# A hybrid transformer trunk on one core: VectorE and ScalarE in written order, with lower parts, conv taps and output copies placed later

## The chip, the cores and the metric

The kernel runs on one core of one Trainium2 chip. The metric is the device time of one execution in microseconds (us), taken as the median of several runs. TensorE multiplies matrices; VectorE, ScalarE and GpSimd work element by element; SyncE issues the loads. A matmul writes into one of eight PSUM banks, all other tiles are in SBUF.

## The reference, cut to what matters

A trunk of two layers on 16 meta tokens and 256 tokens (272 columns), model width 1024, all float32. Each layer is feed-forward, mixer, feed-forward, each with a norm before and after it. The mixer of layer 0 is a gated short convolution, that of layer 1 differential attention.

```python
def swiglu(h, w_gu, w_down):
    g, u = jnp.split(h @ w_gu, 2, axis=-1)        # w_gu 1024 x 5632
    return (jax.nn.silu(g) * u) @ w_down          # w_down 2816 x 1024

def short_conv_mixer(h, w_in, conv_w, w_out):
    b, c, xt = jnp.split(h @ w_in, 3, axis=-1)
    u = causal_conv_of_width_3(c * xt, conv_w)    # per channel
    return (b * u) @ w_out

for i in range(2):
    f = swiglu(rms_norm(h, ln_ffn1[i, 0]), ffn1_w_gu[i], ffn1_w_down[i])
    h = h + 0.5 * rms_norm(f, ln_ffn1[i, 1])
    hn = rms_norm(h, ln_mix[i, 0])
    m = short_conv_mixer(hn, ...) if i == 0 else diff_attention_mixer(hn, ...)
    h = h + rms_norm(m, ln_mix[i, 1])
    f = swiglu(rms_norm(h, ln_ffn2[i, 0]), ffn2_w_gu[i], ffn2_w_down[i])
    h = h + 0.5 * rms_norm(f, ln_ffn2[i, 1])
return h[:, 16:]
```

## The kernel before

Activations lie transposed: 8 tiles of 128 features by 272 columns. The stages follow one another as `f0` (feed-forward), `cv` (conv), `f1`, `f2`, `at` (attention), `f3`. Each has an input projection (streams `guf0`, `cin`, `guf1`, `guf2`, `qkv`, `guf3`) and an output projection (`dnf0`, `cout`, `dnf1`, `dnf2`, `o`, `dnf3`).

**Products.** Every float32 operand is split into a high part in the fast fp32r type and a lower part, x = hi + lo, and a 128 by 128 weight tile times an activation tile is three matmuls: hi·hi, hi·lo, lo·hi (`mm3`, L182; L183 to L185). One such triple is called a product here. `order_up` (L53) sets their order in an input projection: the first 48 products run over k with six outputs open, then every further output takes its eight k in a row.

**Weights.** They come in loads of 16 tiles into three raw buffers (L118). A group is half a load, 8 tiles. `prepare` (L128) makes the group that is next in the queue: ScalarE casts two halves of it to `hi` (L144) and VectorE subtracts to get `lo` (L146). There are seven buffers each for `hi` and `lo` (`HIS`), so group n writes where group n-7 stood and waits until TensorE has read it. `stream` (L166) calls `prepare` once in the middle of every group and, where fewer than four groups are ready or an output projection ends, once more; in the first 50 products of an input projection `Pre.before` (L362) calls it at chosen steps instead.

**Around a norm.** `Post.done` (L316) squares each finished output of an output projection (ScalarE, L289), has the square added up (L293) and copies the output with its gain out of PSUM (L319). `Post.root` (L324) runs two warm matmuls, then multiplies sum and last square by a matrix of ones (`ms_out`, L302), and takes a root on ScalarE (L328); eight more warm matmuls follow, and VectorE makes the stage's first input `z` (L334 to L338). The input projection starts at once, with inputs that are not yet normed. At product 50 (`LATE`) the input norm is there: `inv_sqrt` (L432) has the root `s` on ScalarE (L434) and the reciprocal `rs` on VectorE (L436), and only then can the six open outputs be read by `done`: in a feed-forward gate g (L455), silu on ScalarE (L457), times `rs` on GpSimd (L458), times up on VectorE (L463), split into `a_hi` (ScalarE, L227) and `a_lo` (VectorE, L228). In conv they are c (L489), u (L493), the three taps of y (L495 to L497), times `rs` on GpSimd (L498), cv (L502), split. `Post.h` (L341) makes the residual stream some 24 products later: a reciprocal `rho` on VectorE (L345) and eight GpSimd products `h` (L349). In attention `rotate` (L556) has a shuffle and a product on VectorE and two operations on GpSimd (L562, L563) for q and k of each head; `Head.scores` (L572) makes the weights `w` (L606), and `Head.turn` transposes them on TensorE (L619).

**What sets the order.** TensorE runs in the order written throughout (L94). VectorE and ScalarE are put in order by the scheduler, by priority, with two exceptions: from the first product of an input projection to product 50 they run as written (L366, L392), and `queued` (L124) holds a cast or a subtraction behind the last root or reciprocal. Each engine runs its own list from front to back, whatever that order is.

## Time and profile before

| what | value |
|---|---|
| median of 3 runs | 1067.39 us (1066.76 to 1067.83) |
| profiled execution | 1065.28 us, of which the span of the profile is 1063.5 us |
| mean granted clock of TensorE | 0.994 |
| TensorE busy | 1035.5 us (97%) |
| VectorE busy | 722.8 us (68%) |
| ScalarE busy | 560.8 us (53%) |
| GpSimd busy | 199.2 us (19%) |

PE is TensorE, PEld its weight loads, DVE is VectorE, ACT ScalarE, POOL GpSimd. Times count from the start of the span. A row of a timeline gives start, duration, engine, line, operation, out<-in, shape and count; in brackets stands how long the engine sat idle before it and what released it. PEclk is the granted clock as a share of 2.4 GHz. Buffer numbers and stage digits are left out of names there: `s_f`, `ps_dnf`, `hi_guf` belong to whichever feed-forward is running.

### The profile page before, as it was taken

To read this page: it belongs to the slowest core of one execution; us is meant where nothing else is said; L and a number is where in the kernel's file an instruction comes from. 1 tells how busy PE (TensorE), PEld (TensorE's weight loads), DVE (VectorE), ACT (ScalarE), POOL (GpSimd) and SP (SyncE) were. 2 spreads that over 40 slices of the span, in tenths; PEclk is the share of its full clock that TensorE was granted. 3 is DMA by queue.
4 is the path that set the end of the run, shared out by engine and by line. 5 is a ranking of instruction groups with operands and counts; after the bars stand their busy time and mean duration, and the time that the engine had idled before them with its cause. 6 is when DMAs were issued, how large, how long until landed. Compare 5 with 4: busy or idle time off the path is not lost.

```text
span 1063.5 us, 19962 instructions
## 1 busy us (share of the span) xinstructions
PE 1035.5 (97%) x7948; PEld 1005.5 (95%) x7948; DVE 722.8 (68%) x1427; ACT 560.8 (53%) x1229; POOL 199.2 (19%) x211
## 2 busy tenths in 40 slices
PE   8999999999999999999999999999699989999997
PEld 8999999999999999999999999999689989999886
DVE  6776654488858876644788665448999878876542
ACT  6654444554556554445465444455466666555542
POOL 0211111104121521100034111100712102411000
PEclk9999999999999999999999999999999999999999
DMA  8564454524642564544336554443233424654541
GB/s 309 181 230 173 166 191 160 191 87 158 239 159 80 206 231 158 182 176 161 135 141 227 174 194 159 176 182 119 80 129 113 154 82 158 214 212 173 191 143 40
DMA packets 27022, 176.41 MB, mean 166 GB/s; under 512 B 3120, under 2 KB 4528, under 8 KB 6320
## 3 DMA queue, kind: packets, MB, share of 16 engines
q1 hardware_dynamic: 26784, 175.08, 46.1%
q8 instruction: 62, 1.02, 0.4%
q14 instruction: 32, 0.26, 0.1%
q10 hardware_dynamic: 144, 0.06, 0.0%
HBM read 174.08 MB, written 1.05 MB: 165 GB/s over the span
## 4 chain that ended last, share of the span: by engine, by line
PE 88%; DVE 6%; ACT 2%; POOL 1%; issue 1%; DMA 0%; SPq 0%; DVEq 0%; POOLq 0%
PE ps_guf L185 14%; PE ps_guf L183 14%; PE ps_guf L184 14%; PE ps_dnf L183 6%; PE ps_dnf L184 6%; PE ps_dnf L185 6%; PE ps_guf L207 2%; PE ps_guf L209 2%; PE ps_guf L211 2%; PE ps_out L727 2%; PE ps_out L725 2%; PE ps_out L726 2%; PE ps_qkv L183 1%; DVE lo_cin L146 1%; PE ps_qkv L184 1%
## 5 line engine op out<-in xcount | busy, mean ns | idle before, releaser
L185 PE MATMUL ps_guf<-x_f_hi,lo_guf 128*128 128x272 f32 (+1 forms) x1216 | 349.0, 287 | 0.6 <-DVE lo_guf L146 0.6
L183 PE MATMUL ps_guf<-x_f_hi,hi_guf 128*128 128x272 f32 (+1 forms) x1216 | 349.4, 287 | 0.0
L184 PE MATMUL ps_guf<-x_f_lo,hi_guf 128*128 128x272 f32 (+1 forms) x1216 | 347.6, 286 | 0.0
L144 ACT CAST hi_guf<-raw_guf 128x512 fp32r<-128x512 f32 x349 | 198.1, 615 | 127.6 <-PE ps_guf L184 53.7
L146 DVE TENSOR_TENSOR lo_guf<-raw_guf,hi_guf 128x512 fp32r<-128x512 f32 x349 | 236.7, 717 | 31.9 <-ACT hi_guf L144 25.9
L184 PEld LDWEIGHTS ps_guf<-x_f_lo,hi_guf 128*128 128x128 f32 x1216 | 230.7, 190 | 0.1
L185 PEld LDWEIGHTS ps_guf<-x_f_hi,lo_guf 128*128 128x128 f32 x1216 | 228.5, 188 | 0.8 <-DVE lo_guf L146 0.8
L183 PEld LDWEIGHTS ps_guf<-x_f_hi,hi_guf 128*128 128x128 f32 x1216 | 228.8, 188 | 0.1
L146 DVE TENSOR_TENSOR lo_dnf<-raw_dnf,hi_dnf 128x512 fp32r<-128x512 f32 x176 | 114.1, 689 | 102.1 <-ACT hi_dnf L144 99.8
L458 POOL TENSOR_TENSOR sg_f<-sg_f,rs_f 128x272 f32<-128x272 f32 (+1 forms) x88 | 91.9, 1048 | 454.9 <-ACT sg_f L457 454.9
L144 ACT CAST hi_dnf<-raw_dnf 128x512 fp32r<-128x512 f32 x176 | 100.8, 619 | 129.6 <-PE ps_dnf L184 50.6
L183 PE MATMUL ps_dnf<-a_f_hi,hi_dnf 128*128 128x272 f32 x528 | 152.2, 288 | 0.0
L185 PE MATMUL ps_dnf<-a_f_hi,lo_dnf 128*128 128x272 f32 x528 | 152.1, 288 | 0.0
L184 PE MATMUL ps_dnf<-a_f_lo,hi_dnf 128*128 128x272 f32 x528 | 151.7, 287 | 0.0
L184 PEld LDWEIGHTS ps_dnf<-a_f_lo,hi_dnf 128*128 128x128 f32 x528 | 100.0, 189 | 0.0
L183 PEld LDWEIGHTS ps_dnf<-a_f_hi,hi_dnf 128*128 128x128 f32 x528 | 99.4, 188 | 0.0
L185 PEld LDWEIGHTS ps_dnf<-a_f_hi,lo_dnf 128*128 128x128 f32 x528 | 99.2, 188 | 0.0
L463 DVE TENSOR_TENSOR av_f<-ps_guf,sg_f 128x272 f32<-128x272 f32 (+1 forms) x88 | 38.4, 436 | 75.9 <-PE ps_guf L185 55.8
L455 DVE TENSOR_TENSOR g_f<-ps_guf,rs_f 128x272 f32<-128x272 f32 (+1 forms) x88 | 37.4, 433 | 34.1 <-PE ps_guf L185 34.1
L227 ACT CAST a_f_hi<-av_f 128x272 fp32r<-128x272 f32 (+1 forms) x88 | 36.4, 414 | 33.0 <-DVE av_f L463 32.9
L293 POOL TENSOR_TENSOR acc_out_f<-acc_out_f,sq_out_f 128x272 f32<-128x272 f32 x21 | 18.0, 859 | 162.2 <-ACT sq_out_f L289 162.2
L457 ACT ACTIVATE sg_f<-g_f 128x272 f32<-128x272 f32 (+1 forms) x88 | 36.8, 424 | 19.8 <-DVE g_f L455 19.8
(291 smaller groups left out, 1789.8 us busy)
## 6 DMA issues: line engine op xcount, KB each, us to landing
raw_guf<-in_guf SPq DMA_DIRECT2D x85, 1024.0 KB, 4.8
raw_dnf<-in_dnf SPq DMA_DIRECT2D x44, 1024.0 KB, 4.8
raw_cin<-in_cin SPq DMA_DIRECT2D x12, 1024.0 KB, 4.8
raw_qkv<-in_qkv SPq DMA_DIRECT2D x12, 1024.0 KB, 4.8
raw_cout<-in_cout SPq DMA_DIRECT2D x4, 1024.0 KB, 4.8
raw_o<-in_o SPq DMA_DIRECT2D x4, 1024.0 KB, 4.8
raw_guf<-in_guf SPq DMA_DIRECT2D x6, 384.0 KB, 5.4
h<-in_xT SPq DMA_DIRECT2D x8, 136.0 KB, 4.7
```

Source lines behind the costliest of these rows:

```text
L144: nc.scalar.copy(hi[:, sl], both[:, sl])
L146: nc.vector.tensor_tensor(lo[:, sl], both[:, sl], hi.bitcast(F32)[:, sl], ALU.subtract)
L183: nc.tensor.matmul(o, whi, xhi, start=start, stop=False)
L184: nc.tensor.matmul(o, whi, xlo, start=False, stop=False)
L185: nc.tensor.matmul(o, wlo, xhi, start=False, stop=stop)
L207: nc.tensor.matmul(o, hi, xhi, start=start, stop=False)
L209: nc.tensor.matmul(o, lo, xhi, start=False, stop=False)
L227: nc.scalar.copy(hi, x)
L455: nc.vector.tensor_tensor(g[:, :n], p, pre.r, ALU.mult)
L457: nc.scalar.activation(s[:, :n], g[:, :n], AF.Silu)
L458: nc.gpsimd.tensor_tensor(s[:, :n], s[:, :n], pre.r, ALU.mult)
L463: nc.vector.tensor_tensor(v[:, :n], p, keep.pop(j)[:, :n], ALU.mult)
```

## The change

`hold()` puts VectorE and ScalarE in written order from the first product of `f0` on; `let_go()` gives them back to the scheduler only at product 50 of attention, and `hold()` takes them again 16 products before the end of `o`. `prepare` loses its `queued` waits, and the mid-group call now runs only if fewer than six groups are ahead. `done` takes outputs that end together by rank (all gates ahead of the ups; in conv all c, then u, then b). `a_lo` is issued three products later (`later`, `run_later`), the conv taps behind y two products later. In `o` all squares come first, and the copies out of PSUM follow: two behind the sixth square, one between the mean and the root, five behind the root.

```diff
+    def hold():
+        if not held:
+            held.append(tc.manual_schedule(engines={mybir.EngineType.DVE, mybir.EngineType.Activation}))
+            held[0].__enter__()
+
+    def let_go():
+        if held:
+            held.pop().__exit__(None, None, None)
+
+    def run_later(now=None):
+        while later and (now is None or later[0][0] <= now):
+            later.pop(0)[1]()
@@ prepare
-                with queued(last["sqrt"]):
-                    nc.scalar.copy(hi[:, sl], both[:, sl])
-                with queued(last["rs"]):
-                    nc.vector.tensor_tensor(lo[:, sl], both[:, sl], hi.bitcast(F32)[:, sl], ALU.subtract)
+                nc.scalar.copy(hi[:, sl], both[:, sl])
+                nc.vector.tensor_tensor(lo[:, sl], both[:, sl], hi.bitcast(F32)[:, sl], ALU.subtract)
@@ stream
+            now[0] += 1
+            run_later(now[0])
-            elif j == HC // 2:
+            elif j == HC // 2 and ahead(label, i) < HIS - 1:
                 prepare()
@@ project
-                for e in ended:
+                for e in sorted(ended, key=lambda e: rank(e[0])):
                     done(*e)
@@ split
-            nc.vector.tensor_tensor(lo, x, hi.bitcast(F32), ALU.subtract)
+            later.append((now[0] + 3, lambda: nc.vector.tensor_tensor(lo, x, hi.bitcast(F32), ALU.subtract)))
@@ Post.root
             self.ms = self.norm.mean()
+            if self.copies:
+                self.copies.pop(0)()
...
             warm(WARM_B, f"b_{self.name}")
+            for copy in self.copies:
+                copy()
@@ Pre.before
-                    self.order = ExitStack()
-                    self.order.enter_context(tc.manual_schedule(engines={mybir.EngineType.DVE, mybir.EngineType.Activation}))
+                    run_later()
+                    hold()
...
                 self.ready()
-                self.order.close()
+                if self.name == "at":
+                    let_go()
@@ conv, done
-                nc.vector.scalar_tensor_tensor(y[:, 1:], u[:, : T - 1], CW(1, j), y[:, 1:], ALU.mult, ALU.add)
-                nc.vector.scalar_tensor_tensor(y[:, 2:], u[:, : T - 2], CW(0, j), y[:, 2:], ALU.mult, ALU.add)
-                nc.gpsimd.tensor_tensor(y, y, pre.r, ALU.mult)
+                def taps():
...
+                if now[0] > start[0] + LATE + 1:
+                    later.append((now[0] + 2, taps))
+                else:
+                    taps()
@@ attention, o
+            if i == len(ORD_O) - 16:
+                hold()
...
-                    post.done(e, place(e))
+                    post.square(e, place(e))
+                    if e == KD - 3:
+                        for e in range(2):
+                            post.copy(e, place(e))
+        post.copies = [lambda m=m: post.copy(m, place(m)) for m in range(2, KD)]
```

The lists of TensorE and SyncE are the same before and after. Three places on the others follow; names end in a buffer number.

ScalarE at the end of `f0`, from the square of the seventh output (`sq_out_f0_7`) to the root of the output norm (`sz_f0`), before:

```order
L289 ACTIVATE sq_out_f0_7_2529<-ps_dnf0_6_2448 128x272
L319 ACTIVATE f_f0_6_2532<-ps_dnf0_6_2448,half2_115 128x272
L144 CAST hi_cin_2_0_2581<-raw_cin_2_2579 128x512 x2
L144 CAST hi_cin_2_1_2605<-raw_cin_2_2579 128x512 x2
L144 CAST hi_cin_3_0_2619<-raw_cin_3_2617 128x512 x2
L289 ACTIVATE sq_out_f0_8_2637<-ps_dnf0_7_2534 128x272
L319 ACTIVATE f_f0_7_2639<-ps_dnf0_7_2534,half2_115 128x272
L328 ACTIVATE sz_f0_2650<-ms_out_f0_2647 128x272
```

and after:

```order
L308 ACTIVATE sq_out_f0_7_2528<-ps_dnf0_6_2447 128x272
L344 ACTIVATE f_f0_6_2531<-ps_dnf0_6_2447,half2_115 128x272
L161 CAST hi_cin_1_0_2542<-raw_cin_1_2540 128x512 x2
L161 CAST hi_cin_1_1_2566<-raw_cin_1_2540 128x512 x2
L161 CAST hi_cin_2_0_2580<-raw_cin_2_2578 128x512 x2
L161 CAST hi_cin_2_1_2604<-raw_cin_2_2578 128x512 x2
L308 ACTIVATE sq_out_f0_8_2628<-ps_dnf0_7_2533 128x272
L344 ACTIVATE f_f0_7_2630<-ps_dnf0_7_2533,half2_115 128x272
L355 ACTIVATE sz_f0_2639<-ms_out_f0_2636 128x272
```

The cast of `cin` group 3_0 has left its place ahead of the last square; it comes now in the first steps of conv.

ScalarE in `f0` behind product 50, from the root of the input norm (`s_f0`) on, before:

```order
L434 ACTIVATE s_f0_416<-ms_in_f0_414 128x272
L144 CAST hi_guf0_4_0_463<-raw_guf0_4_461 128x512
L264 ACT_TABLE_LOAD
L264 ACTIVATE junk_140<-s_f0_416 128x1
L144 CAST hi_guf0_4_0_463<-raw_guf0_4_461 128x512
L144 CAST hi_guf0_4_1_493<-raw_guf0_4_461 128x512
```

and after:

```order
L466 ACTIVATE s_f0_416<-ms_in_f0_414 128x272
L283 ACT_TABLE_LOAD
L283 ACTIVATE junk_140<-s_f0_416 128x1
L489 ACTIVATE sg_f0_0_426<-g_f0_0_424 128x272
L489 ACTIVATE sg_f0_1_431<-g_f0_1_429 128x272
L489 ACTIVATE sg_f0_2_436<-g_f0_2_434 128x272
L246 CAST a_f0_0_hi_441<-av_f0_0_439 128x272
L246 CAST a_f0_1_hi_446<-av_f0_1_444 128x272
L246 CAST a_f0_2_hi_451<-av_f0_2_449 128x272
L161 CAST hi_guf0_4_0_459<-raw_guf0_4_457 128x512 x2
L489 ACTIVATE sg_f0_3_482<-g_f0_3_480 128x272
L161 CAST hi_guf0_4_1_492<-raw_guf0_4_457 128x512 x2
```

The casts of groups 4_0 and 4_1 (the ninth and tenth of the stage) stood right behind the root and stand now behind three silus and three splits.

GpSimd in attention behind product 50, from its first operation there, before:

```order
L349 TENSOR_TENSOR h_f2_0_9477<-f_f2_0_8328,rho_f2_9475 128x272
L349 TENSOR_TENSOR h_f2_1_9479<-f_f2_1_8414,rho_f2_9475 128x272
L349 TENSOR_TENSOR h_f2_2_9481<-f_f2_2_8508,rho_f2_9475 128x272
L349 TENSOR_TENSOR h_f2_3_9483<-f_f2_3_8600,rho_f2_9475 128x272
L562 TENSOR_TENSOR rot_q_0_9299<-rot_q_0_9299,sr_8998 128x256
L562 TENSOR_TENSOR rot_k_0_9305<-rot_k_0_9305,sr_8998 128x272
L563 TENSOR_TENSOR q_0_9301<-q_0_9301,rot_q_0_9299 128x256
L562 TENSOR_TENSOR rot_q_1_9313<-rot_q_1_9313,sr_8998 128x256
L349 TENSOR_TENSOR h_f2_4_9485<-f_f2_4_8694,rho_f2_9475 128x272
L563 TENSOR_TENSOR k_0_9307<-k_0_9307,rot_k_0_9305 128x272
```

and after:

```order
L601 TENSOR_TENSOR rot_q_0_9281<-rot_q_0_9281,sr_8980 128x256
L601 TENSOR_TENSOR rot_k_0_9287<-rot_k_0_9287,sr_8980 128x272
L601 TENSOR_TENSOR rot_q_1_9295<-rot_q_1_9295,sr_8980 128x256
L602 TENSOR_TENSOR q_0_9283<-q_0_9283,rot_q_0_9281 128x256
L602 TENSOR_TENSOR k_0_9289<-k_0_9289,rot_k_0_9287 128x272
L602 TENSOR_TENSOR q_1_9297<-q_1_9297,rot_q_1_9295 128x256
```

All eight `h` of the residual stream stand now behind q and k of heads 0 to 2, and VectorE's reciprocal `rho` (L345), which they need and which stood right behind `rs`, stands behind the scores of head 0.

## Rows read from the trace of the kernel before

**Rows 1.** The page: the chain of work that ended last, by engine.

```profile
PE 88%; DVE 6%; ACT 2%; POOL 1%; issue 1%; DMA 0%; SPq 0%; DVEq 0%; POOLq 0%
```

**Rows 2.** Windows, f0 in steady state: us; busy PE, PEld, DVE, ACT, POOL; PEclk; DMA; GB/s.

```profile
45.00:205.00 160.00, 160.00 (x1278) 160.00 (x1277) 94.44 (x167) 82.26 (x165) 26.08 (x25) 1.00 0.54 190
```

**Rows 3.** Timeline, end of f0: ScalarE, then TensorE.

```profile
210.04 1.14 ACT L144 CAST hi_cin<-raw_cin 128x512 fp32r<-128x512 f32 x2 [1.86 <-PE ps_dnf L184]
211.09 0.39 ACT L289 ACTIVATE sq_out_f<-ps_dnf 128x272 f32<-128x272 f32 x1
...
211.53 0.73 PE L302 MATMUL ms_out_f<-sq_out_f,ones 128*128 128x272 f32 x2 [0.70 <-ACT sq_out_f L289]
```

**Rows 4.** Timeline, end of cout's input: VectorE, then TensorE.

```profile
289.35 0.44 DVE L502 TENSOR_TENSOR cv<-ps_cin,y 128x272 f32<-128x272 f32 x1 [0.95 <-POOL y L498]
...
290.29 0.39 PE L183 MATMUL ps_cout<-a_cv_hi,hi_cout 128*128 128x272 f32 x1 [0.83 <-ACT a_cv_hi L227]
291.40 0.39 PE L184 MATMUL ps_cout<-a_cv_lo,hi_cout 128*128 128x272 f32 x1 [0.71 <-DVE a_cv_lo L228]
```

**Rows 5.** Timeline, f0 behind product 50: TensorE, ScalarE, VectorE, GpSimd, TensorE.

```profile
29.59 0.29 PE L183 MATMUL ps_guf<-x_f_hi,hi_guf 128*128 128x272 f32 x1
...
29.42 0.40 ACT L434 ACTIVATE s_f<-ms_in_f 128x272 f32<-128x272 f32 x1 [7.80 <-PE ms_in_f L302]
...
36.50 0.42 ACT L227 CAST a_f_hi<-av_f 128x272 fp32r<-128x272 f32 x1 [0.31 <-DVE av_f L463]
36.82 1.14 ACT L144 CAST hi_guf<-raw_guf 128x512 fp32r<-128x512 f32 x2
...
29.85 1.85 DVE L436 RECIPROCAL rs_f<-s_f 128x272 f32<-128x272 f32 x1 [6.22 <-ACT s_f L434]
...
41.12 1.28 DVE L146 TENSOR_TENSOR lo_guf<-raw_guf,hi_guf 128x512 fp32r<-128x512 f32 x2
...
33.29 2.70 POOL L458 TENSOR_TENSOR sg_f<-sg_f,rs_f 128x272 f32<-128x272 f32 x3 [30.88 <-ACT sg_f L457]
...
38.52 0.39 PE L185 MATMUL ps_guf<-x_f_hi,lo_guf 128*128 128x272 f32 x1 [0.60 <-DVE lo_guf L146]
```

**Rows 6.** Timeline, conv behind product 50: ScalarE's root, VectorE's taps.

```profile
233.39 0.40 ACT L434 ACTIVATE s_cv<-ms_in_cv 128x272 f32<-128x272 f32 x1 [4.29 <-PE ms_in_cv L302]
...
238.83 0.91 DVE L496 SCALAR_TENSOR_TENSOR y<-u,gains,y 128x271 f32<-128x271 f32 x2
```

**Rows 7.** Timeline, attention behind product 50: VectorE, GpSimd, TensorE.

```profile
752.60 2.03 DVE L146 TENSOR_TENSOR lo_qkv<-raw_qkv,hi_qkv 128x512 fp32r<-128x512 f32 x2
...
746.11 3.27 POOL L349 TENSOR_TENSOR h_f<-f_f,rho_f 128x272 f32<-128x272 f32 x4 [33.45 <-DVE rho_f L345]
...
748.41 0.39 PE L183 MATMUL ps_qkv<-x_at_hi,hi_qkv 128*128 128x272 f32 x1 [1.26 <-DVE q L561]
754.13 1.76 PE L582 MATMUL pss<-k,q 64*128 64x144 f32 x8 [2.44 <-POOL k L563]
769.41 0.33 PE L619 MATMUL pw<-ident,w 128*128 128x128 f32 x1 [3.60 <-DVE w L606]
```

**Rows 8.** Windows: attention behind product 50, its later part, and the passage to f3.

```profile
740.00:750.00 10.00, 8.74 (x69) 8.44 (x69) 8.55 (x19) 7.18 (x13) 3.89 (x5) 1.00 0.28 105
750.00:760.00 10.00, 7.56 (x52) 6.56 (x51) 8.31 (x17) 1.66 (x4) 9.92 (x11) 0.83 0.18 59
790.00:830.00 40.00, 40.00 (x309) 36.42 (x308) 39.42 (x118) 25.28 (x85) 10.06 (x12) 1.00 0.38 133
860.00:870.00 10.00, 6.54 (x38) 5.36 (x38) 7.28 (x17) 6.26 (x18) 0.00 (x0) 0.83 0.31 108
```

**Rows 9.** Timeline, passage to f3: ScalarE's copies and squares, TensorE; last row, VectorE's tail.

```profile
859.54 0.51 ACT L319 ACTIVATE f_at<-ps_o,gains 128x256 f32<-128x256 f32 x1
...
865.22 0.70 PE L302 MATMUL ms_out_at<-acc_out_at,ones 128*128 128x256 f32 x2 [3.46 <-DVE acc_out_at L293]
...
1057.77 0.69 DVE L733 TENSOR_TENSOR y_out<-ps_out,g_out 128x512 f32<-128x512 f32 x1 [1.28 <-ACT sq_out L732]
```

More of the change, by code (lines that the diff above doesn't have):

```diff
@@ L94, in trunk_kernel @@
     ctx.enter_context(tc.manual_schedule(engines={mybir.EngineType.PE}))
+    held = []
+    def hold():
[5 more added lines that the diff above has]
+            held.pop().__exit__(None, None, None)
+    ctx.callback(let_go)
+    later = []
+    def run_later(now=None):
+        while later and (now is None or later[0][0] <= now):
+            later.pop(0)[1]()
     def bank(name):
@@ L159, in ahead @@
         return done - c - 1
+    now = [0]
     base, taken = {}, 0
@@ L185, in mm3, with project @@
         nc.tensor.matmul(o, wlo, xhi, start=False, stop=stop)
-    def project(label, nk, xs, cols, done, pre=None):
+    def project(label, nk, xs, cols, done, pre=None, rank=lambda m: 0):
         open_, count, ended, held = {}, {}, [], []
@@ L316, in done, with square, copy @@
         def done(self, m, p):
+            self.square(m, p)
+            self.copy(m, p)
+        def square(self, m, p):
             self.norm.add(p)
+        def copy(self, m, p):
             f = state.tile([P, T], F32, tag=f"f{m}", name=f"f_{self.name}_{m}")
@@ L329, in root @@
             warm(WARM_B, f"b_{self.name}")
+            for copy in self.copies:
+                copy()
+        copies = ()
         def z(self, hk, k, hi=None):
@@ L464, in done @@
                 acts.append(split(v[:, :n], f"ah{j}", f"al{j}", f"a_{name}_{j}", n))
-        project(f"gu{name}", KD, pre.xs, lambda m: c0, done, pre)
+        project(f"gu{name}", KD, pre.xs, lambda m: c0, done, pre, lambda m: m // KF)
         if post_g is None:
@@ L476, in conv @@
         r2 = tmp.tile([P, T], F32, tag="r2", bufs=1, name=f"r2_{name}")
-        keep, acts = {}, []
+        keep, acts, start = {}, [], [now[0]]
         def ready():
@@ L495, in done @@
                 nc.scalar.activation(y, u, AF.Copy, scale=CW(2, j))
-                nc.vector.scalar_tensor_tensor(y[:, 1:], u[:, : T - 1], CW(1, j), y[:, 1:], ALU.mult, ALU.add)
-                nc.vector.scalar_tensor_tensor(y[:, 2:], u[:, : T - 2], CW(0, j), y[:, 2:], ALU.mult, ALU.add)
-                nc.gpsimd.tensor_tensor(y, y, pre.r, ALU.mult)
                 keep[KD + j] = y
+                def taps():
+                    nc.vector.scalar_tensor_tensor(y[:, 1:], u[:, : T - 1], CW(1, j), y[:, 1:], ALU.mult, ALU.add)
+                    nc.vector.scalar_tensor_tensor(y[:, 2:], u[:, : T - 2], CW(0, j), y[:, 2:], ALU.mult, ALU.add)
+                    nc.gpsimd.tensor_tensor(y, y, pre.r, ALU.mult)
+                if now[0] > start[0] + LATE + 1:
+                    later.append((now[0] + 2, taps))
+                else:
+                    taps()
             else:
@@ L503, in done @@
                 acts.append(split(v, f"ah{j}", f"al{j}", f"a_{name}_{j}", T))
-        project("cin", KD, pre.xs, lambda m: 0, done, pre)
+        project("cin", KD, pre.xs, lambda m: 0, done, pre, lambda m: (m // KD - 1) % 3)
         post = Post(name, GM(0, 1), 0)
```

## The prediction, as it was put on record

> **What bounds the kernel now.** I read the chain of waits first: 88% of it is TensorE [rows 1]. The windows say what that means in a steady stage: over 160 us of f0 TensorE is never idle, 1278 matmuls in 160.00 us, 0.125 us each and 0.376 us a product of three, while VectorE has 94 us of work and ScalarE 82 us [rows 2]. In such a stretch another order of those two changes nothing: about 60 us of slack on each hides it, provided that no group is late. So only the stretches count where TensorE stands still. I listed its timeline by idle time; they are the ends of four output projections [rows 3], the end of conv's input [rows 4], the time behind product 50 in f0 [rows 5] and attention [rows 7], and the passage to f3 [rows 9]. The clock comes from the windows [rows 8]: behind some of these it falls.
>
> **The ends of four output projections (f0, cv, f1, f2).** Before, the cast of group 3_0 stands on ScalarE ahead of the last square. It waits 1.86 us for the buffer of the group that TensorE uses last, so it starts at 210.04, when that projection is through, and the square starts behind it at 211.09 [rows 3]. TensorE waits for the square: the second `ms_out` matmul starts at 211.53 after 0.70 idle [rows 3]; the four places read alike. With the cast gone the square can start at about 210.2, when the last matmul is out, 0.85 earlier; the cast, moved into the first steps of conv, takes the place of another one there. **Gain 4 x 0.85 = 3.4** (3.0 to 3.9).
>
> **The end of conv's input.** Before, VectorE waits 0.95 us for GpSimd's y ahead of cv of the last output, and its split is late for `cout` twice: 0.83 and 0.71 idle [rows 4], 1.95 us with the restart of the pipeline. With taps and lower parts two and three products later, a subtraction fills what was waited for, and this is over before `cout` asks. **Gain 1.9** (0 to 2.0).
>
> **Behind product 50 in f0: the price of a written order.** Eight groups are ready there, so TensorE needs the ninth at product 64 and the tenth at 72. Product 51 starts at 29.59, 0.17 behind the root [rows 5], so these are due at 34.5 and 37.5. Before, the ninth's cast stood right behind the root. Now it stands behind the third `a_hi`, whose chain runs over four engines: root until 29.82, reciprocal 1.85 until 31.6, one g and one silu (0.42 each, like the split) until 32.5, three GpSimd products 2.70 until 35.2, av and `a_hi` 0.42 each until 36.07, and half a cast (1.14 for two) until 36.6 [rows 5]. That is 2.1 late; half a lo (1.28 for two [rows 5]) adds 0.4. Then three lower parts, a g and a silu stand ahead of the tenth's cast: 1.28 + 1.1 + 0.4 + 0.4 + 0.57 puts it at 40.4, due by then at 40.0, and 0.4 more for its lo. Together 3.3, against 0.8 before (0.60 idle at 38.52 [rows 5] and the restart). **Loss 2.6** (1.5 to 3.6).
>
> **The same in conv.** Nine groups are ready (one more than in f0), and the tenth is due at product 72: 233.39 + 0.17 + 21 x 0.376 = 241.45. Its cast stands behind the second `a_cv_hi`: root and reciprocal to 235.6, then r2, two c and u (0.36 each), the taps of two outputs (0.91 for two, four of them [rows 6]) with the ScalarE step between, GpSimd, cv, split, half a cast: 242.6 to 243.1. No stall before. **Loss 2.0** with the lo (1.2 to 2.6).
>
> **The same in f1, f2 and f3.** Nine groups are ready there too; the tenth comes 7.2 us behind the root (36.6 - 29.4) and is due at 8.06. The eleventh comes 3.8 later, with its lo at 11.6, due at 11.3. **Loss 0.3 each in f1 and f2, 0.4 in f3** where a product has 256 columns, 1.0 in all (0 to 1.8). Later groups have 3 us each and are made in 2.6, so the lag shrinks.
>
> **Attention.** Before, four of the `h` products run on GpSimd from 746.11 for 3.27 us ahead of the first rotation; then TensorE waits 1.26 for q, 2.44 for k, and 3.60 for w, which comes last [rows 7]. All eight `h` and their reciprocal move behind. q and k then come before TensorE asks. But w is VectorE's, and VectorE is busy 8.55 and 8.31 of the next two 10 us, then 39.42 of 40 [rows 8]: its work is only moved, so what is won is its idle time, 3.1 us, less about 0.5, plus a little where a subtraction no longer runs beside GpSimd. The waits for q and k become a longer wait for w. **Gain 3.0** (0 to 6, the sum of the first two waits with a shorter third).
>
> Two subtractions beside a busy GpSimd took 2.03 [rows 7] and two beside an idle one 1.28 [rows 5]. The `h` products now run beside such a pair ahead of w; I count them at the 2.03. The Trainium skill (SBUF — State Buffer, Who interferes with whom) has it harsher: a VectorE instruction with two SBUF inputs and a GpSimd one that reads SBUF exclude each other for a whole instruction. By that the pair would take 1.28 + 2 x 0.82 = 2.9 and the gain would be 2.1; the rows show about half of it, so I keep mine.
>
> **The passage to f3.** Before, every output has a square and a copy on ScalarE, the eighth square comes at the end of both, and TensorE waits until 865.22 [rows 9]. Eight copies at some 0.36 (0.51 with its overlap [rows 9]) lie among the squares; three stay ahead of the root. The sum of squares is ready 2.7 earlier; five copies behind the root hold banks that TensorE asks for, 0.6. **Gain 2.1** (1 to 3.5). In the window around it the clock is 0.83, which is 3.4 us at the lower level, 1.2 GHz [rows 8]. With 2.7 less of 3.46 us idle I expect none: the nearest wait that short, 1.26 at 748.41, left the window at 1.00, and 2.44 at 754.13 came with 0.83 [rows 7, 8]. About 11 matmuls fall into it, at 0.1 each. **Gain 1.0** (0 to 1.7).
>
> **The clock behind the new stalls.** f0 and conv now have idle times of about 1.9 and 1.5, between those two rows and nearer to the short one: I take no fall. If it falls, each costs half of 3.4, **1.7** (so 0 to 3.4).
>
> **The tail.** The small step to the root of the last rows stands now behind the last y_out, 0.69 [rows 9]. **Loss 0.5**, straight on the end.
>
> **Sum.** 3.4 + 1.9 - 2.6 - 2.0 - 1.0 + 3.0 + 2.1 + 1.0 - 0.5 = 5.3 us. The profiled execution took 1065.28, so this becomes 1060.0; the median is 2.1 above that execution, so I forecast **1062** for the median. A measurement tells about 0.2% from no change, 2.1 us here.
>
> **Rivals.**
>
> *VectorE takes the gain back in attention.* If its work ahead of w only changes its order, w comes at 769 as before, the 3.0 are gone: 1065.0; with one fall of the clock 1066.7. For it: 39.42 of 40 busy. Against it: 3.1 us idle ahead of that [rows 8].
>
> *Head of line at every norm: slower.* Place: the cast behind the last split, in five stages. The chain of 7.2 us has 0.85 to spare in f1 and f2. It decides from about 8.2 on, which a first GpSimd product of 1.2 (a rate of 2.70 for three gives 0.9) and subtractions at 1.0 (2.03 for two) would reach. Then f0 loses 1.5 more, conv 1.0, f1, f2 and f3 1.2 each, and the clock falls behind f0's and conv's stall, 3.4: 6.1 + 3.4 = 9.5, **1071.5**. For it: strict order leaves no way round. Against it: VectorE is idle while GpSimd works in that chain, since its next operation waits for it.
>
> *The stalls are half as long.* GpSimd at 0.7 instead of 0.9 a product takes 0.6 from each chain, and the tenth and eleventh groups come in time: f0, conv and the rest lose 3.2 instead of 5.6; with 3 more in attention 5.4: **1056.6**. Against it: attention's bound.
>
> **How the numbers follow.** Forecast 0.48 (1059.5 to 1064.5), the first rival 0.24, the second 0.13, the third 0.15. Range 1056.5 to 1068.5: it takes in the first rival, two thirds of the third and a part of the second, about 0.8 in all; terms are independent enough that their bounds are not added. Faster by over 0.2% (below 1065.3): 0.48 + 0.15 + a third of the first rival = 0.71. Same: the rest of that, and a little of the second, 0.17. Slower (above 1069.5): 0.12.
>
> **What would show it.** Right: at the four ends the second `ms_out` matmul without idle; no idle time at the start of `cout`; in f0 a wait of about 2 us for the cast of the ninth group, in conv one of 1.5 for the tenth; in attention no wait for q and k, one long wait for w which ends around 764 on the new clock less what was won before; the passage to f3 under 1 us idle with the clock at 1.00. Wrong: groups due on time in f0 and conv (third rival), stalls at every norm with the clock at the lower level behind them (second), w as late as before (first).

## The result, and the profile after

The changed kernel is slower: 1079.89 us as the median of four runs (1078.50 to 1081.31), against 1067.26 for the kernel before in the same rounds. The ratio is 1.0118 [1.0101, 1.0136]. Its profiled execution took 1080.72 us, with a span of 1078.9 us and a mean granted clock of 0.983 (0.994 before). Forecast were 1062 and a range up to 1068.5.

The page after: busy time and share of the span for each engine, and the chain of work that ended last.

```profile
PE 1039.6 (96%) x7948; PEld 1008.7 (93%) x7948; DVE 733.5 (68%) x1427; ACT 556.5 (52%) x1229; POOL 170.0 (16%) x211
...
PE 82%; DVE 11%; ACT 3%; POOL 2%; issue 2%; DMA 1%; SPq 0%; DVEq 0%; ACTq 0%; POOLq 0%
```

The work is the same and VectorE's busy share too, 68%. But VectorE holds 11% of the chain, where it held 6% [rows 1]. Where the time went can be read by laying the first matmul of each stage in the two timelines beside each other (after minus before, us; the span as a whole is 15.4 longer, in a profiled execution that is 0.8 above its median, where that of before was 2.0 below its own):

| stretch | difference | my term |
|---|---|---|
| start, up to product 50 of f0 (its second load lands later in this execution) | +1.2 | - |
| f0 behind product 50 | +3.1 | +2.6 |
| the four ends | -3.6 | -3.4 |
| conv behind product 50 | +2.5 | +2.0 |
| **output projection of conv (`cout`)** | **+7.8** | **-1.9** |
| f1, f2, f3 behind product 50 | +1.9 | +1.0 |
| attention, up to the first product of `o` | -0.5 | -3.0 |
| passage to f3, with f3's first products | -2.9 | -3.1 |
| **output projection of f3 and tail** | **+5.9** | **+0.5** |

Five of the eight terms came out within 1 us, not all of them for the reason given (see below). The loss comes from two places where I had forecast a gain and next to nothing. The next fence is TensorE's timeline after, at the waits that matter (start, duration, then idle time and releaser in brackets).

```profile
37.77 0.39 PE L202 MATMUL ps_guf<-x_f_hi,hi_guf 128*128 128x272 f32 x1 [1.87 <-ACT hi_guf L161]
...
215.04 0.68 PE L321 MATMUL ms_out_f<-sq_out_f,ones 128*128 128x272 f32 x2
...
246.88 0.40 PE L202 MATMUL ps_cin<-x_cv_hi,hi_cin 128*128 128x272 f32 x1 [1.78 <-ACT hi_cin L161]
...
302.42 0.59 PE L202 MATMUL ps_cout<-a_cv_hi,hi_cout 128*128 128x272 f32 x1 [6.98 <-ACT a_cv_hi L246]
...
778.92 0.48 PE L658 MATMUL pw<-ident,w 128*128 128x128 f32 x1 [7.30 <-DVE w L645]
...
874.73 0.70 PE L321 MATMUL ms_out_at<-acc_out_at,ones 128*128 128x256 f32 x2 [1.34 <-DVE acc_out_at L312]
...
1008.63 0.50 PE L770 MATMUL ps_out<-hi_dnf,a_f_hi 128*128 128x512 f32 x1 [1.59 <-DVE g_f L487]
...
1011.43 0.80 PE L770 MATMUL ps_out<-hi_dnf,a_f_hi 128*128 128x512 f32 x1 [1.84 <-DVE e_out L762]
```

The square at the ends no longer holds TensorE up (215.04 without idle, 0.70 before [rows 3]). The waits for a cast in f0 and conv are there (1.87, 1.78). New is `cout`, which stands still for 6.98 us until the split of conv's last output is made; before it was 0.83 and 0.71 [rows 4]. New too are two waits of `dnf3` for PSUM banks: the first lasts until VectorE has read the last gate of f3, the second until it has read that gate's up (`e_out`, named as its releaser, is a memset of 0.06 us that VectorE runs right behind that up).

Where conv's last output hangs is seen on VectorE, after. TensorE ends with that output's inputs at about 292.5.

```profile
293.49 0.43 DVE L541 TENSOR_TENSOR cv<-ps_cin,y 128x272 f32<-128x272 f32 x1
294.40 0.44 DVE L247 TENSOR_TENSOR a_cv_lo<-cv,a_cv_hi 128x272 fp32r<-128x272 f32 x1 [0.49 <-ACT a_cv_hi L246]
...
298.77 0.50 DVE L531 SCALAR_TENSOR_TENSOR y<-u,gains,y 128x271 f32<-128x271 f32 x1 [0.65 <-ACT y L527]
...
301.49 0.43 DVE L541 TENSOR_TENSOR cv<-ps_cin,y 128x272 f32<-128x272 f32 x1
302.40 0.44 DVE L247 TENSOR_TENSOR a_cv_lo<-cv,a_cv_hi 128x272 fp32r<-128x272 f32 x1 [0.48 <-ACT a_cv_hi L246]
```

From cv to cv is 8.00 us, and the last cv starts 9.0 us behind TensorE: VectorE is a whole output late. I call that distance the **lag** from here on: start of VectorE's g (or c, cv) less start of the last matmul of that output, both from the timelines. Behind a norm it is large in both kernels, since VectorE must work off six open outputs at once; what differs is how fast it falls. (us; a round is one gate with its up, or one conv output)

| | peak f1, f2 | fall per round | at the last gate of f2, of f3 | at the last cv |
|---|---|---|---|---|
| before | 6.9 | 1.8 | 0.3, 0.3 | 2.8 |
| after | 11.1 | 0.5 | 4.0, 7.4 | 9.0 |

In conv the fall is 2.0 a round before and 1.0 after. In f3, where products have 256 columns and TensorE's round is 5.7 us, it is 1.55 before and only 0.24 after, so f3 ends with the larger lag.

TensorE takes 6.0 us for a round of f2. VectorE's own round there, after, from g to g, 5.53 us:

```profile
583.53 0.43 DVE L487 TENSOR_TENSOR g_f<-ps_guf,rs_f 128x272 f32<-128x272 f32 x1
585.04 1.45 DVE L162 TENSOR_TENSOR lo_guf<-raw_guf,hi_guf 128x512 fp32r<-128x512 f32 x2 [1.07 <-ACT hi_guf L161]
586.41 0.43 DVE L495 TENSOR_TENSOR av_f<-ps_guf,sg_f 128x272 f32<-128x272 f32 x1
587.33 0.45 DVE L247 TENSOR_TENSOR a_f_lo<-av_f,a_f_hi 128x272 fp32r<-128x272 f32 x1 [0.49 <-ACT a_f_hi L246]
587.85 1.29 DVE L162 TENSOR_TENSOR lo_guf<-raw_guf,hi_guf 128x512 fp32r<-128x512 f32 x2
589.06 0.43 DVE L487 TENSOR_TENSOR g_f<-ps_guf,rs_f 128x272 f32<-128x272 f32 x1
```

and before, at a gate that is still late too, 4.20 us:

```profile
571.49 0.43 DVE L455 TENSOR_TENSOR g_f<-ps_guf,rs_f 128x272 f32<-128x272 f32 x1
571.84 1.28 DVE L146 TENSOR_TENSOR lo_guf<-raw_guf,hi_guf 128x512 fp32r<-128x512 f32 x2
573.78 0.44 DVE L463 TENSOR_TENSOR av_f<-ps_guf,sg_f 128x272 f32<-128x272 f32 x1 [0.67 <-POOL sg_f L458]
574.14 1.28 DVE L146 TENSOR_TENSOR lo_guf<-raw_guf,hi_guf 128x512 fp32r<-128x512 f32 x2
575.34 0.44 DVE L228 TENSOR_TENSOR a_f_lo<-av_f,a_f_hi 128x272 fp32r<-128x272 f32 x1
575.69 0.44 DVE L455 TENSOR_TENSOR g_f<-ps_guf,rs_f 128x272 f32<-128x272 f32 x1
```

And ScalarE over the same round, after:

```profile
584.06 0.43 ACT L489 ACTIVATE sg_f<-g_f 128x272 f32<-128x272 f32 x1 [1.25 <-DVE g_f L487]
584.39 1.13 ACT L161 CAST hi_guf<-raw_guf 128x512 fp32r<-128x512 f32 x2
586.88 0.42 ACT L246 CAST a_f_hi<-av_f 128x272 fp32r<-128x272 f32 x1 [1.35 <-DVE av_f L495]
587.20 1.14 ACT L161 CAST hi_guf<-raw_guf 128x512 fp32r<-128x512 f32 x2
```

The first fence and the last are one loop: g, then silu, then the cast that is written behind it, then its lower part, then av, then `a_hi`, then `a_lo`. Each engine waits for the other once on either half of the round (1.07 and 0.49, 1.25 and 1.35). VectorE has about 4 us of work in 5.53, and no spare time helps it, because the next instruction of its list is never ready early. Over the whole run the group of lower parts shows the same; its last column is the idle time ahead of it. After, then before:

```profile
L162 DVE TENSOR_TENSOR lo_guf<-raw_guf,hi_guf 128x512 fp32r<-128x512 f32 x349 | 241.2, 734 | 90.4 <-ACT hi_guf L161 85.2
```

```profile
L146 DVE TENSOR_TENSOR lo_guf<-raw_guf,hi_guf 128x512 fp32r<-128x512 f32 x349 | 236.7, 717 | 31.9 <-ACT hi_guf L144 25.9
```

### The profile page after: what moved, and what is told of

Its sections match the earlier page's. It is cut to its first block, busy times and chain, and to the rows that moved or that the text cites. A ratio compares the mean times of both kernels' runs of the same rounds, so it can differ in the third digit from the quotient of the medians.

```text
span 1078.9 us, 19950 instructions
## 1 busy us (share of the span) xinstructions
PE 1039.6 (96%) x7948; PEld 1008.7 (93%) x7948; DVE 733.5 (68%) x1427; ACT 556.5 (52%) x1229; POOL 170.0 (16%) x211
## 4 chain that ended last, share of the span: by engine, by line
PE 82%; DVE 11%; ACT 3%; POOL 2%; issue 2%; DMA 1%; SPq 0%; DVEq 0%; ACTq 0%; POOLq 0%
PE ps_guf L204 13%; PE ps_guf L202 13%; PE ps_guf L203 13%; PE ps_dnf L202 6%; PE ps_dnf L204 6%; PE ps_dnf L203 6%; PE ps_guf L226 2%; PE ps_guf L228 2%; PE ps_guf L230 2%; PE ps_out L770 2%; PE ps_out L772 2%; PE ps_out L771 2%; PE ps_qkv L202 1%; DVE lo_cin L162 1%; PE ps_qkv L203 1%
## 5 line engine op out<-in xcount | busy, mean ns | idle before, releaser
L162 DVE TENSOR_TENSOR lo_guf<-raw_guf,hi_guf 128x512 fp32r<-128x512 f32 x349 | 241.2, 734 | 90.4 <-ACT hi_guf L161 85.2
L161 ACT CAST hi_guf<-raw_guf 128x512 fp32r<-128x512 f32 x349 | 195.9, 612 | 9.4 <-DMA raw_guf<-in_guf 4.7
L490 POOL TENSOR_TENSOR sg_f<-sg_f,rs_f 128x272 f32<-128x272 f32 (+1 forms) x88 | 68.5, 783 | 494.4 <-ACT sg_f L489 494.4
L161 ACT CAST hi_dnf<-raw_dnf 128x512 fp32r<-128x512 f32 x176 | 97.1, 623 | 20.7 <-PE ps_out L772 20.7
L247 DVE TENSOR_TENSOR a_f_lo<-av_f,a_f_hi 128x272 fp32r<-128x272 f32 (+1 forms) x88 | 38.9, 450 | 36.7 <-ACT a_f_hi L246 36.7
L308 ACT ACTIVATE sq_out_f<-ps_dnf 128x272 f32<-128x272 f32 x24 | 9.6, 398 | 91.9 <-PE ps_dnf L204 91.9
L202 PE MATMUL ps_qkv<-x_at_hi,hi_qkv 128*128 128x272 f32 (+1 forms) x144 | 44.0, 305 | 0.0
```

Of the source, the lines that this page charges most:

```text
L161: nc.scalar.copy(hi[:, sl], both[:, sl])
L162: nc.vector.tensor_tensor(lo[:, sl], both[:, sl], hi.bitcast(F32)[:, sl], ALU.subtract)
L202: nc.tensor.matmul(o, whi, xhi, start=start, stop=False)
L247: later.append((now[0] + 3, lambda: nc.vector.tensor_tensor(lo, x, hi.bitcast(F32), ALU.subtract)))
L490: nc.gpsimd.tensor_tensor(s[:, :n], s[:, :n], pre.r, ALU.mult)
```

## The experiments

**Theories.** *Lag* (mine, after the result): the order that is written throughout couples VectorE and ScalarE, so that the lag behind each norm is worked off at 0.5 us a round, and `cout` and `dnf3` meet what is left. Rivals: *the delays* (`a_lo` and the taps two or three products later make the last outputs late); *the lead* (casts six groups ahead stand before what `cout` needs); and for attention *the clock* (a slow TensorE sets the pace behind the wait for w). Where the times of the runs are compared with the kernel before, its median in the same rounds was between 1066.64 and 1067.59.

**e1: order given back at every product 50.**

```diff
-                if self.name == "at":
-                    let_go()
+                let_go()
```

> The change with one part undone: VectorE and ScalarE go back to the scheduler at product 50 of every stage, not of attention alone; all the rest of the change stays. Theory 1 (in written order VectorE falls some 11 us behind TensorE at each norm and wins back only 0.3 to 0.6 us in a round of 6, where the free order won back 1.8): the lag drains again, the idle 7.1 us ahead of the last input of cout shrink to under 2, the waits at the start of dnf3 (1.8 and 2.0) and behind product 64 of f0 and 72 of conv go, and what the change wins at the four ends of output projections (0.9 each) and at the passage to f3 (2.1 and 0.8) stays: 1060 to 1062. Theory 2 (the lower parts and taps that are issued later make cout wait): they still are, so cout still waits about 7 and the time is 1069 to 1072.

Measured: 1055.85, ratio 0.9897 [0.9883, 0.9912], 24 us below the changed kernel, and below the range expected, which had left out what the missing `queued` gives (e10). The lag in f1 falls by 1.8 a round, from 8.8 to 0.3 within six gates, and is 1.1 at the last cv. `cout` starts without idle, 1.7 below before; f0, conv and f3 have no wait behind product 50. The group of lower parts waits 23.3 us for casts instead of 85.2 (25.9 before):

```profile
L162 DVE TENSOR_TENSOR lo_guf<-raw_guf,hi_guf 128x512 fp32r<-128x512 f32 x349 | 228.2, 695 | 29.9 <-ACT hi_guf L161 23.3
```

So the written order behind product 50 costs all that was lost, and the rest of the change is worth 1%.

**e2: no delays, order as changed.** `a_lo` and the taps stand at once.

```diff
-            later.append((now[0] + 3, lambda: nc.vector.tensor_tensor(lo, x, hi.bitcast(F32), ALU.subtract)))
+            nc.vector.tensor_tensor(lo, x, hi.bitcast(F32), ALU.subtract)
...
-                if now[0] > start[0] + LATE + 1:
-                    later.append((now[0] + 2, taps))
-                else:
-                    taps()
+                taps()
```

> The change with its delays undone: a_lo and the taps are issued at once, and the written order stays throughout. Theory 1: the written order still has a wait on another engine at every step, so cout waits 5 us or more, dnf3 3 or more, and the time is 1077 to 1083. Theory 2: cout no longer waits, nor does dnf3, and the time is 1067 to 1070.

Measured: 1081.28, ratio 1.0136 [1.0121, 1.0151], not to be told from the changed kernel. The lag is still 6.9 at the last cv and 7.4 at f3's last gate, and `cout` waits 4.89. TensorE in e2:

```profile
303.50 0.45 PE L202 MATMUL ps_cout<-a_cv_hi,hi_cout 128*128 128x272 f32 x1 [4.89 <-ACT a_cv_hi L246]
```

That is 2.1 less than with the delays, but f0 and conv behind product 50 are 2.4 and 1.7 longer than in the changed kernel. The delays move part of the loss from one stage to another; they are not its cause.

**e3: a shorter lead, order as changed.** Extra groups only where fewer than two are ready.

```diff
-AHEAD = 4
+AHEAD = 2
```

> The change with two groups of weights made ahead instead of four (AHEAD 2), so two groups fewer are made behind each norm ahead of the outputs that wait; written order and delays stay. Theory 1 with the lag built up by these groups (2.6 us of VectorE each): the lag peaks 4 to 5 us lower, cout waits about 2 to 3, dnf3 not at all: 1066 to 1071, if no group comes late. Theory 2: cout waits 7 as before, 1079 to 1081.

Measured: 1081.49, ratio 1.0136 [1.0119, 1.0153]; the 1066 to 1071 of my own theory did not come, as its condition, no late group, failed. This one parts the two halves of the loss. With fewer casts to work off, the lag's peak in f1 is 6.9, it is 3.1 at the last cv, `cout` waits 1.09 and `dnf3` not at all. But the fall per round is 0.5 as before, and now weights are late: 4.79 of idle in conv, below, and about 1.9 behind product 50 in each of f1, f2 and f3. TensorE's timeline of e3:

```profile
246.57 0.59 PE L202 MATMUL ps_cin<-x_cv_hi,hi_cin 128*128 128x272 f32 x1 [4.79 <-ACT hi_cin L161]
...
300.94 0.39 PE L202 MATMUL ps_cout<-a_cv_hi,hi_cout 128*128 128x272 f32 x1 [1.09 <-ACT a_cv_hi L246]
```

The lead sets where the coupling is paid for, not whether.

**e4: the kernel before with the new rule for mid-group calls alone.**

```diff
-            elif j == HC // 2:
+            elif j == HC // 2 and ahead(label, i) < HIS - 1:
```

> The kernel before with one line of the change: the call of prepare in the middle of a group only if fewer than six groups are ahead. Both theories: the last square no longer stands behind a cast, 0.9 at each of four ends, nothing elsewhere: 3.5 less than before, 1063.8. If the gain needs the written order as well: 1067.3.

Measured: 1064.22, ratio 0.9973 [0.9964, 0.9983]. The four ends gain 0.9 each, 3.6 in all. So that gain belongs to the rule, not to the order. Elsewhere the rule has effects that I had not expected. The passage to f3 waits 2.21 instead of 3.46 [rows 9], since of the two groups that were cast among the eight squares one has gone; with the clock behind it that is 2.1. Attention loses: from its norm to the first product of `o` it takes 93.42 against 90.69. `cout` loses 0.8.

**e5: order as changed, the loop cut in another place.** The lower part of a weight group is issued four products after its cast.

```diff
+SKEW = 4
...
-    def prepare():
+    def prepare(skew=0):
...
-                nc.vector.tensor_tensor(lo[:, sl], both[:, sl], hi.bitcast(F32)[:, sl], ALU.subtract)
+                sub = lambda sl=sl: nc.vector.tensor_tensor(lo[:, sl], both[:, sl], hi.bitcast(F32)[:, sl], ALU.subtract)
+                if skew:
+                    later.append((now[0] + skew, sub))
+                else:
+                    sub()
@@ stream, two places
-                prepare()
+                prepare(SKEW)
```

> The change with one thing loosened and the written order kept: the subtraction that makes the lower half of a weight group is issued four products after its cast, so that VectorE does not come to it while ScalarE is still at the cast. Theory 1, with the slow draining put down to the waits between the two engines at each step (VectorE waits 1.05 for the cast and 0.47 for a_hi in a round): a round costs VectorE about 4.4 us instead of 5.4 to 5.5, the lag drains by 1.2 or more in a round of 6, cout waits 4 or less and dnf3 not at all: 1070 to 1075. If the draining has another cause (more work on VectorE, GpSimd beside it), rounds stay at 5.4 and the time at 1079 to 1081.

Measured: 1066.84, ratio 0.9994 [0.9984, 1.0003]; about 13 us below the changed kernel with the order still written throughout, and below the 1070 to 1075 expected. The lag falls by 1.8 a round and is 0.8 at the last cv; neither `cout` nor `dnf3` waits. VectorE at conv's last output, e5:

```profile
292.34 0.44 DVE L530 TENSOR_TENSOR u<-ps_cin,c 128x272 f32<-128x272 f32 x1 [0.58 <-PE ps_cin L209]
292.70 1.28 DVE L163 TENSOR_TENSOR lo_cout<-raw_cout,hi_cout 128x512 fp32r<-128x512 f32 x2
293.90 0.50 DVE L536 SCALAR_TENSOR_TENSOR y<-u,gains,y 128x271 f32<-128x271 f32 x1
...
295.88 0.44 DVE L546 TENSOR_TENSOR cv<-ps_cin,y 128x272 f32<-128x272 f32 x1 [0.95 <-POOL y L538]
```

It waits now for TensorE, which is what an engine that keeps up does, and for GpSimd, no longer for ScalarE. So it is not written order as such, but a lower part that is written right behind its cast. What remains are the waits for weights behind the norm (idle 1.87 and 0.51 in f0, 1.77 and 0.39 in conv), with the granted clock at 0.83 from 30 to 50 and from 245 to 255: the six open outputs still stand ahead of the casts there.

**e6: e1, with the end of `o` as before.** No written order there, squares and copies as they come.

```diff
-            if i == len(ORD_O) - 16:
-                hold()
...
-                    post.square(e, place(e))
-                    if e == KD - 3:
-                        for e in range(2):
-                            post.copy(e, place(e))
-        post.copies = [lambda m=m: post.copy(m, place(m)) for m in range(2, KD)]
+                    post.done(e, place(e))
```

> The kernel of e1 (written order given up at product 50) with the end of o as before: each square followed by its copy, no written order in the last 16 products. If the passage to f3 wins what the traces say (2.1 by the earlier sum of squares, 0.8 by the clock), this is 2.5 to 3.0 slower than e1: 1058.3 to 1058.9. If the free order gives it anyway: as e1, 1055.9.

Measured: 1056.89, ratio 0.9904 [0.9889, 0.9919], within the interval of e1 and below the 1058.3 to 1058.9 that my price of the passage gave. In the traces the passage waits 2.21 against 1.47 in e1: squares first is worth 0.7 us there, too little for the runs to tell.

**e7: e1 without the delays**, the edit of e2 on it.

> The kernel of e1 with the lower parts and taps issued at once. If their delay is what takes the two waits ahead of the last input of cout away (1.95 before, none in e1), they come back: 1057.5 to 1058. If it is the smaller lead of prepare or the order of done: as e1, 1055.9.

Measured: 1055.89, ratio 0.9894 [0.9879, 0.9909], the same as e1. The delays give nothing.

**e8: e1 with a busy TensorE ahead of head 0's transposes.** 56 small matmuls of zeros are added, into the bank that the transposes overwrite.

```diff
+                for _ in range(56 if hd == 0 else 0):
+                    nc.tensor.matmul(pw[:, :WARM_N], warmer[:, :P], warmer, start=True, stop=True)
```

> The kernel of e1 with 56 small matmuls of zeros (about 6 us) ahead of head 0's transposes in attention, in the 7.5 us that TensorE waits for w. Theory 3 (what attention wins is given back to the clock: behind that one long wait TensorE runs some 6 us of products at the lower level): the clock stays up, w is not later, and the end of attention comes about 3 us earlier: 1052.5 to 1053.5. If VectorE sets the pace of attention behind w: no change, 1055.9.

Measured: 1057.01, ratio 0.9904 [0.9889, 0.9919], no gain. The windows over attention (us; busy PE, PEld, DVE, ACT, POOL; PEclk; DMA; GB/s) of e8, and then of e1:

```profile
752.00:766.00 14.00, 12.21 (x104) 10.49 (x103) 14.00 (x31) 5.44 (x19) 8.65 (x11) 1.00 0.21 77
```

```profile
752.00:766.00 14.00, 6.22 (x36) 4.99 (x34) 13.57 (x30) 6.41 (x23) 9.04 (x11) 0.68 0.22 79
```

The granted clock is 1.00 instead of 0.68, but the transposes of the second head come only 1.8 us earlier and those of the third 0.2 later (34.2 and 43.8 us behind the norm's `ms_in`, 36.1 and 43.6 in e1). VectorE is busy 14.00 of 14: it sets the pace, and a low clock of TensorE costs nothing there. The clock's theory falls.

**e9: the kernel before with two edits**, the rule of e4 and `prepare` without `queued`; VectorE and ScalarE under the scheduler wherever they were before.

```diff
-                with queued(last["sqrt"]):
-                    nc.scalar.copy(hi[:, sl], both[:, sl])
-                with queued(last["rs"]):
-                    nc.vector.tensor_tensor(lo[:, sl], both[:, sl], hi.bitcast(F32)[:, sl], ALU.subtract)
+                nc.scalar.copy(hi[:, sl], both[:, sl])
+                nc.vector.tensor_tensor(lo[:, sl], both[:, sl], hi.bitcast(F32)[:, sl], ALU.subtract)
...
-            elif j == HC // 2:
+            elif j == HC // 2 and ahead(label, i) < HIS - 1:
```

> The kernel before with two lines of the change alone: prepare without its waits for the root and the reciprocal, and the call in the middle of a group only if fewer than six groups are ahead. No written order behind product 50, no rank, no delays, o as before. If these two carry what e1 wins (its delays gave nothing, its squares first 1.0), this comes to within 1.5 of e6: 1056.5 to 1058.5, without a wait of cout for its last input. If the order in which outputs are taken (rank) is what helps conv: cout waits 2 again and the time is 1059 to 1061.

Measured: 1056.21, ratio 0.9900 [0.9885, 0.9914]: all of e1. The end of f0 and the passage in e9, TensorE:

```profile
209.97 0.68 PE L300 MATMUL ms_out_f<-sq_out_f,ones 128*128 128x272 f32 x2
...
857.04 0.70 PE L300 MATMUL ms_out_at<-acc_out_at,ones 128*128 128x256 f32 x2 [2.21 <-DVE acc_out_at L291]
```

**e10: the kernel before with `prepare` without `queued`, and nothing else.**

> The kernel before with one line: prepare without its waits for the root and the reciprocal. The casts behind product 50 move ahead of the root, into time in which ScalarE waits 4 to 8 us for the norm; so f0 loses its wait of 0.8, conv is some 2 us less behind at its end and cout waits less; the four ends keep their 0.9. 1062 to 1065. If the gain of e1 in conv and attention is not this line's: 1066.5 to 1067.5.

Measured: 1061.56, ratio 0.9950 [0.9934, 0.9967]. The end of f0 keeps its 0.70 of idle and the passage its 3.46. `cout` gains 1.7 over before, f0 behind product 50 0.9, attention 2.1 (88.60 us from the norm to `o`). Beside e4 that makes the account of e9's 9.0 us in the traces. Without `queued`: f0 0.9, `cout` 1.7, attention 2.1 (and 1.1 lost to a single wait in conv, which e9 has not). By the rule: the ends 3.6, the passage and what follows it 2.0, less 1.2 in attention. Together 9.1. (The medians differ by 10.8; the profiled execution of before is 2.0 below its median.)

**e11: e5 with two groups cast ahead of the six open outputs** in f0 and conv.

```diff
+                if self.name in ("f0", "cv"):
+                    prepare()
+                    prepare()
```

> The kernel of e5 (written order throughout, subtractions four products behind their casts) with two groups made ahead of the root at product 50 of f0 and conv. Theory 1 with the stalls behind the norm put down to the place of the cast in the written order: f0's waits (2.0 and 0.7) and conv's (1.9 and 0.6) go, and with f0's the lower clock behind it (1.7): 1066.8 - 6.9, so 1059.5 to 1061. If TensorE waits there for the outputs and not for the weights: 1066 to 1068.

Measured: 1059.99, ratio 0.9934 [0.9919, 0.9949]. The waits behind the norm are gone in both stages. In conv 1.6 of the 4.2 us won are given back at `cout`: the outputs are later by the two groups, the lag at the last cv is 2.5, and `cout` waits again, e11:

```profile
288.63 0.39 PE L207 MATMUL ps_cout<-a_cv_hi,hi_cout 128*128 128x272 f32 x1 [0.49 <-ACT a_cv_hi L251]
289.73 0.39 PE L208 MATMUL ps_cout<-a_cv_lo,hi_cout 128*128 128x272 f32 x1 [0.71 <-DVE a_cv_lo L252]
```

An order that is written as far as in the changed kernel can thus beat the kernel before; this one stays 4 us behind e1 and e9.

**e12: e7 with one group more ahead of attention's product 50**, to win back what the shorter lead costs there.

```diff
-                    for _ in range(MORE_AT.count(k)):
+                    for _ in range(MORE_AT.count(k) + (self.name == "at" and k == 5)):
```

> The kernel of e7 (prepare without its waits, the call in the middle of a group only below six, rank, squares first; no delays, written order given up at product 50) with one more group made in attention's first products, at k = 5. In e9 the smaller lead cost attention 1.2 against e10 (89.8 and 88.6 us from the norm to the first product of o). If that is the group that is missing at product 50, this gives it back: 1054.5 to 1055. If VectorE's work up to w is what counts, whichever group it is for: as e7, 1055.9.

Measured: 1056.39, ratio 0.9898 [0.9882, 0.9915], no gain over e7; attention takes 89.4 us instead of 89.7 in e7, and conv takes 1.0 more, by a single wait of 0.69 for VectorE's c that the edit, which stands in attention, does not explain. The fastest versions, e1, e7 and e9, lie at 1056, about 1% below the kernel before. e9 does it with two small edits.

## Why the prediction was wrong

1. **What bounds the kernel: the step that failed.** "In such a stretch another order of those two changes nothing: about 60 us of slack on each hides it, provided that no group is late." The 60 us are there after as before; the steady window of f0 after reads as [rows 2] did, with VectorE at 97.50 of 160:

```profile
45.00:205.00 160.00, 160.00 (x1278) 160.00 (x1277) 97.50 (x169) 80.83 (x164) 18.61 (x24) 1.00 0.51 186
```

Two things were wrong in the sentence. Slack is not there to be used when two engines with fixed lists wait for each other once a round: the round was 5.53 us with about 4 us of work in it (e5 and e1 take the loop out, and the lag falls 1.8 a round again). And groups of weights are not the only thing that can be late. I followed weights behind product 50 to the third group, saw the lag of the weights shrink, and never asked when the outputs that pile up behind a norm are through. In f0, f1 and f2 late outputs cost nothing: 0.3 to 4.0 us of lag are left, and the output projection asks for the last of its 22 inputs only 21 products, 7.9 us, after its start. Conv has three outputs per round and only eight rounds, and `cout` needs the last one 2.6 us (seven products) after its start; `dnf3` needs banks.

2. **The end of conv's input: a gain of 1.9 became a loss of 7.8.** I took the last round by itself, where the 0.95 of waiting for y indeed went. The lag with which that round is entered was not in my sum. e1, e7 and e9 show a gain of 1.7 where VectorE keeps up, but the delays that I credited with it have no part in it: e7 and e9 are without them, and in e10 the missing `queued` alone gives it.

3. **The tail: 0.5 forecast, 5.9 measured.** Two idle times of 1.59 and 1.84 make 3.4 of it, from f3's lag of 7.4. The window around them has a granted clock of 0.83, so 0.17 / 0.5 x 10 = 3.4 us at the lower of the two levels, 1.2 GHz, an estimated 1.7 more; the late y_out adds about the 0.5 that I gave it.

```profile
1006.00:1016.00 10.00, 6.57 (x22) 4.68 (x21) 5.68 (x12) 7.47 (x20) 0.73 (x1) 0.83 0.37 145
```

4. **Attention: 3.0 forecast, 0.5 measured.** w of the first head did come 2.6 us earlier (25.44 behind the norm's `ms_in`, 28.03 before), with one wait of 7.30 in place of three, as forecast. But that was to be kept to the end, and by the second head only 1.0 is left, because VectorE is full from there on: 13.08 of the 14 us around that wait (last section), 50.66 of the 53 from 790 to 843. This was the first rival's mechanism, one head later. The runs divide it: 2.1 gained without `queued` (e10), 1.2 lost to the shorter lead (e9 against e10).

5. **Right, in part by luck.** Right are the four ends (3.4 against 3.6), though by the rule alone, which e4 shows, and conv behind product 50 (2.0 against 2.5), with the cast named and at the distance worked out. In f1 to f3 the eleventh group's lower part was late as forecast; the size was low, 1.0 against 1.9.

   f0 behind product 50 (2.6 against 3.1; the 2.6 is 3.3 less 0.8, so 2.5) has the right cast, the ninth group's, and two errors that cancel. I had 3.3 for the ninth and the tenth. The ninth cost about 2.3 (1.87 and 0.21 of idle with the restart) and the tenth came in time; the clock, for which I took no fall, added an estimated 1.7. Against e1, which has no wait there, f0 is 4.0 longer.

   The passage with its clock (3.1 against 2.9) came out for a reason that I did not name. The cast that the rule takes away gives 2.1 of it (e4); squares first give 0.7 (e6 against e1), where I had 2.7 for them. That was too much from the start: five copies leave their places ahead of the last square, 1.8 at 0.36 each.

6. **The rivals.** The slower one had the right engine pair and the wrong place: it let the chain of 7.2 us grow at every norm, and no wait of 1 us or more appeared in f1 and f2 behind the norm. It priced 1071.5; the kernel took 8 us more. The third, stalls half as long, had GpSimd nearly right (2.23 for the first three products of f0, 2.70 before [rows 5], about 2.1 in its price) and the tenth group of f0 in time; but stalls of 1.87 and 1.78 and a late eleventh group are not half as long.

## What to carry to other kernels

Before putting two in-order engines in written order, follow one round through both lists: if a result goes back and forth between them, the round takes the length of that loop and not the busy time of either, and moving one producer a few steps ahead of its consumer (e5) cuts it. After a burst, work out how much is worked off per round and what is still late at the stage's end, for everything that the next stage takes from it: inputs and PSUM banks, not weights alone. And when a change bundles an order with small rules, run the rules by themselves: here they were worth 1% and the order cost 2%.

## What the runs showed of the hardware

**The clock.** Granted clock, after, in three windows around a stall (columns as in [rows 2]):

```profile
20.00:45.00 25.00, 22.92 (x167) 22.40 (x167) 14.47 (x28) 11.09 (x25) 3.00 (x4) 0.93 0.37 128
296.00:310.00 14.00, 7.58 (x40) 7.39 (x41) 8.26 (x15) 6.58 (x15) 2.62 (x3) 0.63 0.54 204
772.00:786.00 14.00, 6.64 (x29) 5.17 (x30) 13.08 (x33) 5.64 (x20) 9.88 (x12) 0.63 0.20 77
```

and in two around the other stalls, in conv and at the passage to f3:

```profile
240.00:255.00 15.00, 13.01 (x102) 12.57 (x101) 11.46 (x24) 7.61 (x15) 2.63 (x3) 1.00 0.34 117
870.00:885.00 15.00, 13.14 (x105) 12.23 (x104) 12.50 (x32) 11.16 (x31) 0.00 (x0) 1.00 0.22 80
```

Behind the idle 1.87 in f0 the level of 1.2 GHz lasted 0.07 / 0.5 x 25 = 3.5 us, as it did in [rows 8]; around the idle 6.98 and 7.30 it lasted 0.37 / 0.5 x 14 = 10.4 us. I had priced one fall at 3.4 us whatever the stall. Stalls of nearly one length went both ways: behind 1.78 idle in conv and 1.34 at the passage the full clock stayed, behind 1.87 in f0, where I had forecast no fall, it did not. At the passage of e5 TensorE was idle for 2.73 us and the window from 864 to 874 has 1.00; in e11 it was 2.71, and the window from 855 to 865 has 0.83. So the length of a stall alone does not tell; no run here shows what does.

**GpSimd beside VectorE.** The product of silu and `rs` took 783 ns in the mean after and 1048 before, with the same instructions. Beside no VectorE instruction, or beside one that reads PSUM (a gate's or an up's product) or makes a reciprocal, it takes 0.73 to 0.79 us in either kernel. What makes the difference is a weight group's subtraction, which like the product reads two tiles of SBUF, and which of the two starts first. Before, the subtraction was running already in 73 of the 88 cases, and the product took 1.10 in the mean. After, the product started first in 70 of 88: it took 0.77, and the subtraction behind it 0.86 in place of 0.69. In the two rounds shown above, GpSimd before and after, beside VectorE's pairs at 571.84 (1.28) and 585.04 (1.45):

```profile
572.52 1.23 POOL L458 TENSOR_TENSOR sg_f<-sg_f,rs_f 128x272 f32<-128x272 f32 x1 [4.01 <-ACT sg_f L457]
```

```profile
584.56 0.78 POOL L490 TENSOR_TENSOR sg_f<-sg_f,rs_f 128x272 f32<-128x272 f32 x1 [4.15 <-ACT sg_f L489]
```

So the one that starts second is held up. The pair of 2.03 in [rows 7] fits: it is 0.75 above 1.28, about one such product. The prediction priced two of them for a pair, and so took the row for half of what a whole wait costs. In a round of the changed kernel this costs VectorE 0.17 of its 5.53 us (1.45 against 1.28). It is not what keeps the lag up: in e5 the product takes 1143 ns in the mean, more than before, and the lag falls by 1.8 a round.
